# Seven products per block in another order: the v and gate projections of a gated linear attention layer

## The chip, the cores and the metric

One core of a Trainium2 chip runs the whole program. The metric is the device time of one execution in microseconds; the time before is the median of three runs. Below, PE is TensorE, PEld its weight loads, DVE is VectorE, ACT is ScalarE, POOL is GpSimd and SP is SyncE, which issues most loads.

## The reference, cut to what matters

The model has two layers. The first layer's token mixer is a gated linear attention. Its input projection is one large matrix product, of which the change touches two column ranges, v and the gate, each 1024 columns wide:

```
proj = x @ w_in                       # x: 512 x 1024
q, k, v, gate, gk_lr = split(proj, [hk, 2*hk, 2*hk + hv, 2*hk + 2*hv])
o = rms_norm(gla_chunked(q, k, v, g), norm_w)
y = (o * silu(gate)) @ w_out
```

Everything is float32. The kernel keeps float32 accuracy with three products of rounded parts (high x high, low x high, high x low).

## The kernel before, in words

**Seven products instead of eight.** `gated` computes a 512 x 1024 block (v, then the gate) by a scheme of the Strassen-Winograd kind. Tokens, inner dimension and columns are halved, and seven products of sums of quarters replace eight products of quarters. A product's name is that of its weight operand: b11, b21 and b22 are quarters of the weight (row half, column half), t1 to t4 are sums of quarters. The token operand is a quarter of x (a11, a12, a22) or one of four sums (w1, v2, v3, v4) that `x_forms` makes earlier.

**Banks.** Two pairs of PSUM banks accumulate; in a pair, r = 0 and r = 1 are two blocks of 128 tokens. The table `GATED` lists the products in order, each with its token operand and its pair. After the second half of a product, `update` takes each r from its bank: ACT copies it (`copied`), or DVE adds it to, or subtracts it from, a tile already taken out. Some products go on accumulating over what the bank holds already; the others start the bank anew. Either way PE may not write to a bank before `update` has read it. The finished tiles are v or, through a Silu, the gate.

**Halves.** A product comes in two halves (i = 0 and 2), each with its own 128 x 1024 weight tile: 2 x 2 x 3 = 12 matmuls of 128 x 512. The first mixer has 28 such halves, 14 for v and 14 for the gate. They are numbered 0 to 13 here within each part.

**Weights.** A half's raw weight tile is split by ACT into `wh` (a rounding cast, 1.05 us) and then by DVE into `wl` (the rest, 1.2 us). There are four pairs of `wh` and `wl`, so a half's cast can begin only when the half four places earlier has left PE. The raw tiles come in two kinds. The pool `raws` has three slots, shared with every other weight of the program; `gw` has two. A weight sum is made in place: the raw tile, once split, is added to, either by DVE (b11 + b12) or by a transfer from POOL that adds while it writes (`GATED_SUM`). So t1, t2 and t4 are one gw tile in three states, and b22 and t3 are one raw tile in two states. A raw tile that will be added to keeps its slot until the later product has split it.

**What sets the order.** The code issues the halves in the order of `GATED`, each weight a few halves ahead (`look`); a planner with rough costs (`clk`, `vec`) decides where the other work of the mixer (decays, scores, states) is slipped in. Then a scheduler fixes each engine's queue at build time. At run time each queue is strictly in order: an instruction that waits holds up all behind it on its engine.

## Time and profile before

| | us |
|---|---|
| median of three runs | 1223.05 (1222.7 to 1223.29) |
| the profiled execution itself | 1222.6 |
| its span, first to last instruction | 1220.9 |
| PE busy in the span | 1213.7 |
| v halves, first to last matmul | 58.7 to 109.7 |
| gate halves, first to last matmul | 109.9 to 164.1 |

A row of the timeline gives the start, the duration, the engine, the source line, the operation with the tile it writes and those it reads, and in brackets how long the engine was idle before it and who ended that. PE's matmuls are pipelined: a 128 x 512 one is shown as 0.39 us long, but the next starts 0.227 us after it. So a stall on PE is read from the distance of two starts.

### The profile page before, as it was taken

What the parts mean: (1) busy time and instruction counts of PE and PEld (TensorE: products, weight loads), DVE (VectorE), ACT (ScalarE), POOL (GpSimd) and SP (SyncE); (2) the same over time, 40 slices, a digit from 0 to 9 for tenths busy, and PEclk for the clock granted to TensorE, in tenths of its full rate; (3) what the DMA queues carried; (4) which work ended last, traced back from release to release, by engine and by line L of the source; (5) the groups of instructions that cost most, each with busy time, mean ns of one, the idle gap of its engine ahead of it and who ended that gap; (6) DMA issues with size and microseconds to landing.
All of it is one profiled execution on the core that took longest, in us unless ns stands there. A gap on an engine that the chain in (4) does not pass through costs nothing.

```text
span 1220.9 us, 17195 instructions
## 1 busy us (share of the span) xinstructions
PE 1213.7 (99%) x6501; PEld 1024.4 (84%) x6501; DVE 907.4 (74%) x1515; ACT 609.3 (50%) x1072; POOL 161.6 (13%) x203
## 2 busy tenths in 40 slices
PE   9999999999999999999999999999999999999998
PEld 8888888988888888889888888988988888888886
DVE  6989677687757675766789975688687757775667
ACT  5666663644434443454678555544644433443440
POOL 3030101601100110001242030200520100020000
PEclk9999999999999999999999999999999999999999
DMA  8384642535743554433444351335443853383321
GB/s 233 109 165 110 142 143 82 178 116 129 195 125 87 124 100 121 123 102 89 121 128 131 89 136 36 98 110 156 136 123 100 170 179 94 105 178 91 108 65 69
DMA packets 176275, 149.41 MB, mean 122 GB/s; under 512 B 16870, under 2 KB 140842, under 8 KB 176192
## 3 DMA queue, kind: packets, MB, share of 16 engines
q1 hardware_dynamic: 162464, 116.28, 32.3%
q0 software_dynamic: 12768, 31.37, 13.0%
q8 instruction: 51, 0.84, 0.3%
q10 hardware_dynamic: 960, 0.66, 0.2%
q14 instruction: 32, 0.26, 0.1%
HBM read 129.92 MB, written 5.78 MB: 111 GB/s over the span
## 4 chain that ended last, share of the span: by engine, by line
PE 94%; issue 2%; DVE 1%; DMA 1%; ACT 1%; DVEq 0%; POOL 0%; POOLq 0%; ACTq 0%
PE fm L213 55%; PE tm L213 16%; PE fold L213 15%; PE xT L231 1%; DMA gw<-in_gla_w_in_dram 1%; PE o L213 1%; PE pq L213 1%; PE pg L213 1%; PE vn L213 1%; PE yT L231 1%; PE V L213 0%; PE s L213 0%; PE qs L213 0%; PE ks L213 0%; DVE wl L716 0%
## 5 line engine op out<-in xcount | busy, mean ns | idle before, releaser
L213 PE MATMUL fm<-xh,wh 128*128 128x512 f32 (+2 forms) x1096 | 400.3, 368 | 0.7 <-ACT xh L716 0.7
L213 PE MATMUL fm<-xl,wh 128*128 128x512 f32 (+2 forms) x1096 | 398.5, 366 | 0.0
L213 PE MATMUL fm<-xh,wl 128*128 128x512 f32 (+1 forms) x1072 | 391.4, 367 | 0.0
L716 DVE TENSOR_TENSOR wl<-raw,wh 128x1024 fp32r<-128x1024 f32 (+1 forms) x158 | 196.6, 1246 | 150.8 <-ACT wh L716 150.6
L716 ACT CAST wh<-raw 128x1024 fp32r<-128x1024 f32 (+1 forms) x159 | 164.8, 1038 | 210.5 <-PE fm L213 129.0
L213 PEld LDWEIGHTS fm<-xh,wh 128*128 128x128 f32 (+1 forms) x1096 | 205.3, 188 | 33.9 <-ACT xh L716 0.9
L213 PEld LDWEIGHTS fm<-xl,wh 128*128 128x128 f32 (+1 forms) x1096 | 205.4, 188 | 33.1
L213 PEld LDWEIGHTS fm<-xh,wl 128*128 128x128 f32 x1072 | 201.2, 188 | 33.2
L1019 DVE SCALAR_TENSOR_TENSOR conv<-fm,ffn_cw,conv 128x511 f32<-128x511 f32 x112 | 83.5, 746 | 10.0 <-ACT conv L1017 8.3
L213 PE MATMUL fold<-wh,fh 128*128 128x512 f32 x224 | 87.6, 391 | 0.0
L213 PE MATMUL fold<-wh,fl 128*128 128x512 f32 x224 | 87.2, 389 | 0.0
L213 PE MATMUL fold<-wl,fh 128*128 128x512 f32 x224 | 87.1, 389 | 0.0
L716 ACT CAST wh<-b 128x1024 fp32r<-128x1024 f32 x48 | 50.0, 1054 | 74.2 <-PE fold L213 36.8
L716 DVE TENSOR_TENSOR wl<-b,wh 128x1024 fp32r<-128x1024 f32 x48 | 58.2, 1222 | 22.7 <-ACT wh L716 22.4
L412 POOL DMA_DIRECT2D b<-b x24 | 20.8, 902 | 355.0 <-DVE wl L716 304.5
L1037 ACT ACTIVATE conv<-conv 128x512 f32<-128x512 f32 x44 | 27.8, 631 | 64.3 <-DVE conv L1019 64.3
L1574 DVE SCALAR_TENSOR_TENSOR conv<-fm,gdn_cw,conv 128x511 f32<-128x511 f32 (+2 forms) x72 | 54.1, 790 | 5.1 <-ACT conv L1572 4.6
L213 PEld LDWEIGHTS fold<-wh,fh 128*128 128x128 f32 x224 | 42.0, 188 | 9.6 <-DVE h L1108 1.0
L213 PEld LDWEIGHTS fold<-wh,fl 128*128 128x128 f32 x224 | 42.0, 188 | 8.8
L213 PEld LDWEIGHTS fold<-wl,fh 128*128 128x128 f32 x224 | 42.1, 188 | 8.6
L1019 DVE SCALAR_TENSOR_TENSOR form<-fm,ffn_cw,form 128x511 f32<-128x511 f32 x64 | 47.7, 746 | 1.1
L929 POOL TENSOR_TENSOR h<-h,gb 128x512 f32<-128x512 f32 x16 | 24.5, 1547 | 136.4 <-PE xT L231 135.0
(363 smaller groups left out, 2008.7 us busy)
## 6 DMA issues: line engine op xcount, KB each, us to landing
raw<-in_ffn_w_in_dram SPq DMA_DIRECT2D x88, 512.0 KB, 3.9
raw<-in_gdn_w_in_dram SPq DMA_DIRECT2D x32, 512.0 KB, 4.1
b<-in_ffn_w_out_dram SPq DMA_DIRECT2D x24, 512.0 KB, 6.3
b<-b POOLq DMA_DIRECT2D x24, 512.0 KB, 4.7
raw<-in_ffn_w_out_dram SPq DMA_DIRECT2D x20, 512.0 KB, 3.7
raw<-in_gla_w_in_dram SPq DMA_DIRECT2D x18, 512.0 KB, 4.0
gw<-in_gla_w_in_dram POOLq DMA_DIRECT2D x8, 512.0 KB, 7.7
raw<-in_gla_w_out_dram SPq DMA_DIRECT2D x8, 512.0 KB, 3.6
```

What stands on the lines that cost most here:

```text
L213: t = self.nc.tensor.matmul(out, a, b, start=start, stop=stop, skip_group_check=joined)
L231: t = self.nc.tensor.transpose(out, a, self.ident[:n, :n])
L412: self.nc.gpsimd.dma_start(out, group[src, i][:, cols], accum_op=ALU.add)
L716: return self.nc.scalar.copy(dst_h, src), self.nc.vector.tensor_sub(dst_l, src, dst_h)
L929: nc.gpsimd.tensor_mul(h[hf], h[hf], gb[hf])
L1019: nc.vector.scalar_tensor_tensor(a[:, d:], ps[:, :S - d], tap(2 - d), a[:, d:], ALU.mult, ALU.add)
L1037: nc.scalar.activation(a, a, AF.Gelu)
L1574: self.conv = nc.vector.scalar_tensor_tensor(a[:, d:], ps[:, :S - d], tap(3 - d), a[:, d:], ALU.mult, ALU.add)
```

## The change

The order of the seven products goes from b21, b11, t1, b22, t2, t3, t4 (bank pairs 1, 0, 1, 1, 0, 0, 0) to t1, b11, b22, t2, b21, t3, t4 (pairs 1, 0, 1, 0, 1, 0, 0). The first product is now on the sum b11 + b12. So `gated_load` loads b11 into a raw tile and b12 into the gw tile, DVE adds the former to the latter before the first split, and b11 itself is split from the raw tile. b21 comes fifth, on a raw tile of its own. The upper right result is now b11's bank copied by ACT with b21's bank added by DVE; before, b21's was copied and b11's added.

```
-GATED = (("b21", "a12", 1), ("b11", "a11", 0), ("t1", "w1", 1), ("b22", "v4", 1), ("t2", "v2", 0), ("t3", "v3", 0),
+GATED = (("t1", "w1", 1), ("b11", "a11", 0), ("b22", "v4", 1), ("t2", "v2", 0), ("b21", "a12", 1), ("t3", "v3", 0),
          ("t4", "a22", 0))
...
     def gated_load(self, group, name, i):
...
+        def load(quarter, t):
+            self.nc.sync.dma_start(t.rearrange("p (j f) -> p j f", j=2), self.gated_rows(group, quarter, i))
+            group[quarter, i] = t
+
+        raw = lambda: self.rp.tile([P, 1024], F32, name=self.uid("raw"), tag="raw")
+        if name == "t1":
+            load("b11", raw())
+            load("b12", self.mp.tile([P, 1024], F32, name=self.uid("gw"), tag="gw", bufs=2))
+        elif name in ("b22", "b21"):
+            load(name, raw())
 
     def issue_gated(self, group, name, i):
         nc = self.nc
         t = group[GATED_IN[name], i]
         if name == "t1":
-            nc.vector.tensor_add(t, t, group.pop((name, i)))
+            nc.vector.tensor_add(t, t, group["b11", i])
...
-        if name in ("b21", "t3", "t4"):
+        if name in ("b11", "b21", "t3", "t4"):
             del group[GATED_IN[name], i]
...
-            if name == "b21":
-                top[r] = copied(x)
+            if name == "t1":
+                high[r] = copied(x)
             elif name == "b11":
-                nc.vector.tensor_add(top[r], top[r], p)
-                done(r, 1, top[r], top[r])
-            elif name == "t1":
-                high[r] = copied(x)
+                top[r] = copied(p)
...
+            elif name == "b21":
+                nc.vector.tensor_add(top[r], top[r], x)
+                done(r, 1, top[r], top[r])
```

Of PE's queue, the matmuls are the same in kind and number. The queues of DVE and ACT are rearranged from the end of the q and k projections to the output projection. Two places matter for what follows.

The first is DVE's queue in the v part, from the split of half 8 on. There, `na`, `z`, `bc` and the `e` tiles belong to the decays of a head; `wl` rows are splits; `v` rows with `fold` are `update`. Before, half 8 and 9 are t2's (gw), 10 and 11 are t3's (raw):

```order
L716 TENSOR_TENSOR wl_911<-gw_661,wh_910 128x1024
L1360 SCALAR_TENSOR_TENSOR na_905<-z_904 128x512
L1364 SCALAR_TENSOR_TENSOR z_904<-z_904,na_905 128x512
L1366 SCALAR_TENSOR_TENSOR bc_949<-reset_83,z_904 128x512
L716 TENSOR_TENSOR wl_932<-gw_709,wh_931 128x1024
L1371 TENSOR_TENSOR e_176_951<-bc_949 128x512
L716 TENSOR_TENSOR wl_957<-raw_775,wh_956 128x1024
```

Now half 8 and 9 are b21's, both on raw tiles (raw_869 and raw_892):

```order
L717 TENSOR_TENSOR wl_915<-raw_869,wh_914 128x1024
L1361 SCALAR_TENSOR_TENSOR na_909<-z_908 128x512
L1365 SCALAR_TENSOR_TENSOR z_908<-z_908,na_909 128x512
L1367 SCALAR_TENSOR_TENSOR bc_951<-reset_83,z_908 128x512
L1372 TENSOR_TENSOR e_178_953<-bc_951 128x512
L717 TENSOR_TENSOR wl_935<-raw_892,wh_934 128x1024
L717 TENSOR_TENSOR wl_959<-raw_757,wh_958 128x1024
```

The same seven kinds of rows stand there; one split now reads a tile, raw_892, whose load can be issued only when the slot of raw_869 is free, that is behind the first row, since b22's two raw tiles hold the other two slots until t3 is split. A little further on, DVE's queue before ends t2's and t3's turns like this (v_966 and v_974 are t2's subtractions, v_921 and v_929 are t3's):

```order
L1235 TENSOR_TENSOR v_966<-v_966,fold_741 128x512
L716 TENSOR_TENSOR wl_1005<-gw_661,wh_1004 128x1024
L1235 TENSOR_TENSOR v_974<-v_974,fold_742 128x512
L716 TENSOR_TENSOR wl_1025<-gw_709,wh_1024 128x1024
L1394 TENSOR_TENSOR e_185_995<-e_185_995,qk_655 128x4x64
L1395 TENSOR_TENSOR e_185_995<-e_185_995,qk_601 128x4x64
L1360 SCALAR_TENSOR_TENSOR na_1074<-z_1073 128x512
L1397 TENSOR_TENSOR bc_949<-bc_949,qk_601 128x512
L1238 TENSOR_TENSOR v_921<-v_921,fold_741 128x512
```

Now b21's additions (v_877 and v_885) stand in that place, t2's subtractions have gone up the queue, and t3's (v_784, v_792) follow:

```order
L717 TENSOR_TENSOR wl_1005<-gw_611,wh_1004 128x1024
L1390 COPY dec_1000<-bc_951 128x4
L1236 TENSOR_TENSOR v_877<-v_877,fold_747 128x512
L1236 TENSOR_TENSOR v_885<-v_885,fold_748 128x512
L717 TENSOR_TENSOR wl_1027<-gw_615,wh_1026 128x1024
L1394 TENSOR_TENSOR e_184_992<-e_184_992,qk_659 128x512
L1395 TENSOR_TENSOR e_185_995<-e_185_995,qk_659 128x4x64
L1396 TENSOR_TENSOR e_185_995<-e_185_995,qk_601 128x4x64
L1239 TENSOR_TENSOR v_784<-v_784,fold_745 128x512
```

Two rows of the decays (`na`, and `bc` times q) moved behind t3's subtractions, and two `v` rows came in ahead of them.

The second place is ACT's queue in the gate part, at halves 8 to 10 and the copies of the transposed keys (`kt`), which PE's `ds` matmuls read. Before, with t2's halves on gw tiles:

```order
L716 CAST wh_1326<-gw_1063 128x1024
L1220 COPY sg_1337<-fold_1214 128x512
L1220 COPY sg_1345<-fold_1215 128x512
L716 CAST wh_1347<-gw_1129 128x1024
L716 CAST wh_1433<-raw_1246 128x1024
L1425 COPY kt_1399<-kt_1394 128x512
```

Now, with b21's halves on raw tiles, raw_1290 and raw_1314:

```order
L717 CAST wh_1328<-raw_1290 128x1024
L1221 COPY sg_1338<-fold_1218 128x512
L1221 COPY sg_1346<-fold_1219 128x512
L717 CAST wh_1348<-raw_1314 128x1024
L717 CAST wh_1433<-raw_1228 128x1024
L1426 COPY kt_1399<-kt_1394 128x512
```

The `kt` copies stand, as before, behind the casts of halves 9 and 10; the cast of half 9 now reads a tile whose load is issued only after DVE's split of half 8 (raw_1290 to `wl`).

More of the change, by code (lines that the diff above doesn't have):

```diff
@@ L32 @@
 FOLD = [(n, FOLD_NEW[n], *FOLD_ALL[n]) for n in ("b11", "b21", "t1", "t2", "b22", "t3", "t4")]
-GATED = (("b21", "a12", 1), ("b11", "a11", 0), ("t1", "w1", 1), ("b22", "v4", 1), ("t2", "v2", 0), ("t3", "v3", 0),
+GATED = (("t1", "w1", 1), ("b11", "a11", 0), ("b22", "v4", 1), ("t2", "v2", 0), ("b21", "a12", 1), ("t3", "v3", 0),
          ("t4", "a22", 0))
-GATED_NEW = {"b21": "b21", "b11": "b11", "t1": "b12", "b22": "b22"}
-GATED_IN = {"b21": "b21", "b11": "b11", "t1": "b11", "b22": "b22", "t2": "b11", "t3": "b22", "t4": "b11"}
+GATED_IN = {"t1": "b12", "b11": "b11", "b22": "b22", "t2": "b12", "b21": "b21", "t3": "b22", "t4": "b12"}
 GATED_SUM = {"t1": "b22", "b22": "b12", "t2": "b21"}
@@ L438, in gated_load @@
     def gated_load(self, group, name, i):
-        if name not in GATED_NEW:
-            return
-        if name == "b11":
-            t = self.mp.tile([P, 1024], F32, name=self.uid("gw"), tag="gw", bufs=2)
-        else:
-            t = self.rp.tile([P, 1024], F32, name=self.uid("raw"), tag="raw")
-        self.nc.sync.dma_start(t.rearrange("p (j f) -> p j f", j=2), self.gated_rows(group, GATED_NEW[name], i))
-        group[name, i] = t
+        def load(quarter, t):
[7 more added lines that the diff above has]
+            load(name, raw())
     def issue_gated(self, group, name, i):
```

## The prediction

> **What bounds the kernel now.** I read the page's busy times and chain first, then the two parts that the change touches as windows, then what PE waited for in them.

> ```profile
> span 1220.9 us, 17195 instructions
> PE 1213.7 (99%) x6501; PEld 1024.4 (84%) x6501; DVE 907.4 (74%) x1515; ACT 609.3 (50%) x1072; POOL 161.6 (13%) x203
> PE 94%; issue 2%; DVE 1%; DMA 1%; ACT 1%; DVEq 0%; POOL 0%; POOLq 0%; ACTq 0%
> ...
> 58.00:112.00 54.00, 53.61 (x280) 44.33 (x279) 47.69 (x81) 36.65 (x66) 11.06 (x13) 1.00 0.66 150
> 112.00:164.00 52.00, 51.42 (x283) 42.65 (x282) 41.83 (x103) 35.10 (x64) 7.09 (x6) 1.00 0.46 102
> ...
> PE fold L213 <- DVE sg L1235: 0.4, 1, 0.4
> PE fold L213 <- DVE v L1235: 0.4, 1, 0.4
> ```

> PE is the bound: 99% busy, and 94% of the chain that ended last. The windows (length, then PE, PEld, DVE, ACT, POOL busy, clock, DMA share) show the v part and the gate part: the granted clock is 1.00, PE is idle for 0.39 and 0.58 us, and DVE is the next busiest with 47.69 of 54 and 41.83 of 52. The last two rows are all that PE is shown to have waited for there: DVE's subtraction of t2's bank, once in each part. Since PE's work stays the same, the change can win only PE's stalls in these two parts and lose only what it adds to them.

> **What it removes.** PE's rows around the four places where a half must wait for a bank of its own pair (v: t2 to t3, t1 to b22; gate: t1 to b22, t2 to t3):

> ```profile
> 79.53 0.39 PE L213 MATMUL fold<-wh,xfl 128*128 128x512 f32 x1
> 79.77 0.50 PE L213 MATMUL fold<-wh,xfh 128*128 128x512 f32 x1
> 80.11 0.40 PE L213 MATMUL fold<-wl,xfh 128*128 128x512 f32 x1
> ...
> 89.42 0.39 PE L213 MATMUL z<-lr,gk 96*128 96x512 f32 x1
> 90.20 0.47 PE L213 MATMUL fold<-wh,xfh 128*128 128x512 f32 x1 [0.39 <-DVE v L1235]
> 90.51 0.40 PE L213 MATMUL fold<-wl,xfh 128*128 128x512 f32 x1
> ...
> 126.03 0.39 PE L213 MATMUL fold<-wh,xfl 128*128 128x512 f32 x1
> 126.56 0.50 PE L213 MATMUL fold<-wh,xfh 128*128 128x512 f32 x1
> 126.90 0.40 PE L213 MATMUL fold<-wl,xfh 128*128 128x512 f32 x1
> ...
> 150.35 0.71 PE L231 MATMUL yT<-ident,sg 128*128 128x128 f32 x5
> 151.50 0.50 PE L213 MATMUL fold<-wh,xfh 128*128 128x512 f32 x1 [0.43 <-DVE sg L1235]
> 151.83 0.39 PE L213 MATMUL fold<-wl,xfh 128*128 128x512 f32 x1
> ```

> Steps between starts are 0.227 us where nothing waits (rows of 0.39 overlap). Three rows span two steps, 0.45: 79.53 to 80.11 has 0.13 too much, 89.42 to 90.51 has 0.63, 126.03 to 126.90 has 0.41. Behind the transposes, 0.43 idle and 0.33 instead of 0.23 make about 0.6 with the slow first steps. In the new order another product stands between each of these pairs, so the wait has 5.4 us of other matmuls (24 x 0.227) for cover. The sum is 1.8 us, all of it on PE's path. The new queue of PE has one `ds` matmul on its own ahead of t4's first half, one more change between the two kinds; the row at 134.69 further down shows such a first matmul behind `ds` as 0.58 long instead of 0.39, so I put it at 0.2. Net 1.6 us to win, no more: t3 to t4 stays in one pair.

> **What hides at no cost.** The sum b11 + b12 is made before half 0 now; its raw tile is loaded where b21's was.

> ```profile
> 50.47 1.22 DVE L716 TENSOR_TENSOR wl<-raw,wh 128x1024 fp32r<-128x1024 f32 x1
> ...
> 58.70 0.39 PE L213 MATMUL fold<-wh,xh 128*128 128x512 f32 x1
> ```

> Before, the split of half 1 ended at 51.7, and PE began half 0 at 58.70: 7 us of cover for two additions of the same width, 2.4 us. If that cover were gone, each 1 us of lateness would be 1 us of PE. The adding transfers on POOL get one product more between the split that frees them and their use. Evictions are equal in number: ACT copies as often, DVE adds as often.

> **What it adds: a load that stands behind a split.** b21 comes while b22's two raw tiles hold two of three slots. So its second half's load is issued on SP only when DVE has split the first, and that split needs half 4 to have left PE. For v, the rows of before that stand at this point:

> ```profile
> 75.67 1.05 ACT L716 CAST wh<-gw 128x1024 fp32r<-128x1024 f32 x1 [1.67 <-PE fold L213]
> ...
> 76.75 1.22 DVE L716 TENSOR_TENSOR wl<-gw,wh 128x1024 fp32r<-128x1024 f32 x1 [1.49 <-ACT wh L716]
> 80.37 0.69 DVE L1364 SCALAR_TENSOR_TENSOR z<-z,na 128x512 f32<-128x512 f32 x1 [1.79 <-ACT na L1362]
> 81.10 1.22 DVE L1366 TENSOR_TENSOR_SCAN bc<-reset,z 128x512 f32<-128x512 f32 x1
> 82.24 1.20 DVE L716 TENSOR_TENSOR wl<-gw,wh 128x1024 fp32r<-128x1024 f32 x1
> 83.36 0.68 DVE L1371 TENSOR_TENSOR e<-bc 128x512 f32<-128x512 f32 x1
> 83.96 1.22 DVE L716 TENSOR_TENSOR wl<-raw,wh 128x1024 fp32r<-128x1024 f32 x1
> 94.72 0.68 DVE L1238 TENSOR_TENSOR v<-v,fold 128x512 f32<-128x512 f32 x1
> ...
> 95.77 0.39 PE L213 MATMUL fold<-wh,xh 128*128 128x512 f32 x1
> ```

> Half 8 is cast at 75.67 and split by 76.75 + 1.22 = 77.97, now as before. The load goes out at 78.0 and lands L later; ACT's cast takes 1.05, so DVE can start half 9's split at 79.1 + L. DVE itself gets to that row at 82.84: z at 80.37, then 0.73, 1.14 and 0.60 (the distances z to scan, scan to the next, and e to the next). So DVE's queue, and all behind it, is late by L - 3.7. From z to t3's first subtraction DVE ran without a gap (80.37 to 94.72, 14.35 us), and the new queue has the same sum: two 512-wide rows of the decays out, two of `update` in. So t3's subtraction ends at 94.72 + 0.68 + (L - 3.7), and t4, in the same pair, cannot start before. PE would be there at 95.77 - 0.13 - 0.63 + 0.43 (`ds` moved ahead; three of them take 1.21 from 133.48 on, below) = 95.44, where the subtraction of before ended at 95.40: no slack; with 0.1 for the hand-over, **wait A is L - 3.6.**

> L is read from the transfers of 512 KB around (median us to landing; windows at 59, 85, 88.5, 118 and 77 to 79 us):

> ```profile
> raw<-in_gla_w_in_dram SPq DMA_DIRECT2D x1, 512.0 KB, 3.5
> ...
> raw<-in_gla_w_in_dram SPq DMA_DIRECT2D x1, 512.0 KB, 5.6
> ...
> raw<-in_gla_w_in_dram SPq DMA_DIRECT2D x1, 512.0 KB, 4.8
> ...
> raw<-in_gla_w_out_dram SPq DMA_DIRECT2D x1, 512.0 KB, 6.7
> ...
> gw<-in_gla_w_in_dram POOLq DMA_DIRECT2D x1, 512.0 KB, 8.5
> ```

> A load alone took 3.5; one issued while an adding transfer of POOL was under way took 4.8 to 6.7. At 78.0 t2's two adding transfers are under way (issued behind the splits of halves 6 and 7, and taking up to 8.5), so I take 5.6, the row with the most alike neighbours, and keep 3.5 and 6.7 as ends. A is 2.0, from 0 to 3.1. Half 9 itself is in time: split by 85.9 with L = 5.6, needed at 86.6 (one half, 12 x 0.227, before the 89.3 of t3 that is worked out below). [...]

> In the gate part the same load stands ahead of the `kt` copies on ACT.

> ```profile
> 123.54 0.39 PE L213 MATMUL fold<-wh,xfh 128*128 128x512 f32 x1
> ...
> 131.90 1.05 ACT L716 CAST wh<-raw 128x1024 fp32r<-128x1024 f32 x1 [3.03 <-PE fold L213]
> 132.85 1.07 ACT L1425 COPY kt<-kt 128x512 f32<-128x512 f32 x2
> ...
> 133.48 1.56 PE L213 MATMUL ds<-v,kt 128*128 128x256 f32 x6
> 134.69 0.58 PE L213 MATMUL fold<-wh,xfl 128*128 128x512 f32 x1
> ```

> Half 4 leaves PE at 123.54. Cast and split take 1.05 and 1.22, the hand-overs some 0.3 (an estimate), so the load is issued at 126.1 and lands at 126.1 + L. Two casts follow, 0.95 apart (131.90 to 132.85), then `kt` at 128.05 + L. Before it was at 132.85, less half 6's 0.41 that is gone: 132.44. PE's `ds` stands right behind that copy already (it began at 133.48, 0.1 late by the steps). **Wait B is L - 4.4**: 1.2 with 5.6, from 0 to 2.3. In the gate part eight transposes stand between t3 and t4 on PE, so A is not repeated there.

> **The sum:** -1.8 + 0.2 + 2.0 + 1.2 = +1.6 us. On the profiled execution's 1222.6 that is 1224.2; the median of the runs shown lies 0.45 above it, so 1224.6.

> **The rivals.**
> *The loads come quickly* (L up to 4.4, near the lone 3.5): A is 0 to 0.8, B nothing, and the time is 1221.4 to 1222.3. For it: one of the two adding transfers may be nearly through at 78. Against it: every load beside one took 4.8 or more. 25%. [...]
> *The loads come slowly*, the other side: by the sum, +2L - 9.6, the kernel is slower by more than 2.4 us from L = 6.0 on. With 6.7 it is -1.6 + 3.1 + 2.3 = +3.8, so 1226.9. For it: a 6.7 row, at the start of a bunch of POOL's transfers, and two of them under way here. 25%.
> *It does not do what it says:* the waits for banks stay, because DVE's queue puts t2's subtractions late wherever the product stands. They stand behind two splits now, so the first starts at 82.84 + 1.9 + 2 x 1.13 = 87.0 and ends at 87.7; PE needs it at 89.3 (90.20 less 0.55, 0.13 and the `z` matmul's 0.23, which moves behind t3). That is 1.6 us of cover, so against it. Then the 1.8 stays and A and B come on top: +3.4, 1226.4; 5%.
> *Something gives more than these waits:* no row of the two parts holds more; 5% for a gain over 2.4.

> **How the numbers follow.** 0.2% of 1223.05, 2.4 us, is about what a measurement tells from no change. The forecast (L from 4.4 to 6.0, 1222.3 to 1225.5) has 40%. No change is that and the quick loads, 0.65; slower is the slow loads and the waits that stay, 0.30; faster 0.05. The range goes from a gain of the full 1.8, less the 0.3 by which runs differ (1220.9), to the slow loads' 1226.9 with the 0.2 of spread (1227.1).

> **What would show it.** In the profile after: no wait of PE for the t2 subtraction; a wait of PE for DVE's subtraction of t3's bank at t4 in v, near 95.4 to 97.5 us; DVE idle ahead of half 9's split near 83 us, ended by a cast; ACT idle ahead of the cast of half 9 in the gate part near 131 us, ended by a load; PE waiting for `kt`. The prediction is wrong if b21's second load lands within 4 us, or if another row, at half 0 or at the states of t4, becomes a wait.

## The result: 9 us slower, and the profile after

The changed kernel takes 1232.15 us (median of five, 1230.83 to 1233.14) against 1223.05 (also of five): ratio 1.0074, 95% interval 1.0063 to 1.0086. The forecast was 1224.6, its range 1220.9 to 1227.1. The profiled execution is the one of 1232.15 us. First its page: span, busy times, chain.

```profile
span 1230.4 us, 17192 instructions
PE 1217.4 (99%) x6501; PEld 1028.2 (84%) x6501; DVE 907.3 (74%) x1515; ACT 609.3 (50%) x1072; POOL 161.2 (13%) x203
PE 96%; DVE 2%; DMA 1%; ACT 1%; issue 0%; DVEq 0%; POOL 0%; ACTq 0%; POOLq 0%
```

The span is 9.5 us longer, yet PE counts only 3.7 us more of busy time. The page can't tell more; the two parts can. The windows of the v part and the gate part:

```profile
58.00:112.00 54.00, 52.05 (x266) 43.12 (x265) 43.23 (x63) 31.99 (x52) 10.49 (x12) 0.97 0.62 139
112.00:164.00 52.00, 47.47 (x249) 39.48 (x248) 36.12 (x104) 31.99 (x65) 4.72 (x4) 0.93 0.44 105
```

PE is idle for 1.95 and 4.53 us (0.39 and 0.58 before), and the granted clock, 1.00 in both before, is 0.97 and 0.93. Both matter. What PE waited for from 58 to 164 us, all of it (total, times, longest):

```profile
PE ds L212 <- DVE sc L1442: 4.5, 1, 4.5
PE fold L212 <- DVE v L1239: 1.9, 1, 1.9
```

The waits for t2's subtractions are gone, as the change promised. Two new ones stand in their place, and both come from one cause: b21's second load. First the v part, in the timeline:

```profile
83.78 2.00 ACT L717 CAST wh<-raw 128x1024 fp32r<-128x1024 f32 x2 [3.27 <-DMA raw<-in_gla_w_in_dram]
...
84.86 2.36 DVE L717 TENSOR_TENSOR wl<-raw,wh 128x1024 fp32r<-128x1024 f32 x2 [1.64 <-ACT wh L717]
...
96.88 1.28 DVE L1239 TENSOR_TENSOR v<-v,fold 128x512 f32<-128x512 f32 x2
...
95.17 0.59 PE L212 MATMUL ds<-v,kt 128*128 128x256 f32 x2
97.71 0.47 PE L212 MATMUL fold<-wh,xh 128*128 128x512 f32 x1 [1.95 <-DVE v L1239]
98.02 0.47 PE L212 MATMUL fold<-wl,xh 128*128 128x512 f32 x1
98.29 0.63 PE L212 MATMUL fold<-wh,xl 128*128 128x512 f32 x1
98.72 0.63 PE L212 MATMUL fold<-wh,xh 128*128 128x512 f32 x1
...
101.34 0.71 PE L212 MATMUL fold<-wh,xh 128*128 128x512 f32 x1
101.89 0.40 PE L212 MATMUL fold<-wl,xh 128*128 128x512 f32 x1
102.13 0.40 PE L212 MATMUL fold<-wh,xl 128*128 128x512 f32 x1
```

This is wait A: ACT waits for the load, DVE for ACT's cast; DVE's queue runs late, t3's subtraction frees its bank at 97.6, and t4 stands until 97.71, 2.2 us longer than a step would be. Then something that the prediction doesn't contain: the steps are 0.43 us instead of 0.227 (98.29 to 98.72) and become 0.24 only at 101.89. Summed over the steps from 97.7 to 101.9, that is 1.6 us more.

The gate part:

```profile
137.95 1.99 ACT L717 CAST wh<-raw 128x1024 fp32r<-128x1024 f32 x2 [7.68 <-DMA raw<-in_gla_w_in_dram]
...
139.02 1.23 DVE L717 TENSOR_TENSOR wl<-raw,wh 128x1024 fp32r<-128x1024 f32 x1 [4.96 <-ACT wh L717]
139.84 1.06 ACT L1426 COPY kt<-kt 128x512 f32<-128x512 f32 x2
...
140.28 0.44 DVE L1442 COPY_PREDICATED sc<-gla_mask,sa 64x256 f32<-64x256 uint8 x1
...
140.84 0.29 PEld L212 LDWEIGHTS ds<-v,kt 128*128 128x128 f32 x1 [4.94 <-ACT kt L1426]
140.87 0.77 PE L212 MATMUL ds<-v,kt 128*128 128x256 f32 x1 [4.53 <-DVE sc L1442]
...
143.99 0.63 PE L212 MATMUL fold<-wh,xfh 128*128 128x512 f32 x1
144.42 0.63 PE L212 MATMUL fold<-wl,xfh 128*128 128x512 f32 x1
```

This is wait B: 4.7 us more than a step. The weight load of `ds` waits for ACT's `kt` copy, as foreseen; the matmul also waits for DVE's last `sc` copy, which stands behind half 9's split and reads a bank that `ds` needs. Of the two, `sc` ends last: the first of the two `kt` copies, the one that `ds` starts on, ends at 140.42, `sc` at 140.72. Both stand behind the same load. The steps are 0.43 again up to 146.0; that is 2.4 us more.

Now the load itself, as transfers: the answer for 77.5 to 78.5 us (v), that for 129 to 130 us (gate), and the bytes by queue while each load was under way (78.2 to 83.8, 129.3 to 137.9):

```profile
raw<-in_gla_w_in_dram SPq DMA_DIRECT2D x1, 512.0 KB, 5.6
...
raw<-in_gla_w_in_dram SPq DMA_DIRECT2D x1, 512.0 KB, 8.6
...
DMA packets 577, 1.08 MB, mean 193 GB/s; under 512 B 48, under 2 KB 48, under 8 KB 577
...
q0 software_dynamic: 305, 0.56, 62.0%
q1 hardware_dynamic: 272, 0.52, 24.5%
...
DMA packets 860, 1.64 MB, mean 191 GB/s; under 512 B 64, under 2 KB 64, under 8 KB 859
...
q0 software_dynamic: 587, 1.10, 70.9%
q1 hardware_dynamic: 272, 0.52, 17.8%
```

The same 0.52 MB on SP's queue (q1) took 5.6 us beside 0.56 MB of POOL's adding transfers (q0), and 8.6 us beside 1.10 MB. Averaged over the time of the load, all of it together went at about 192 GB/s both times. Within that time it is uneven: up to 81.0 us in v and 132.3 us in the gate part, 2.8 and 3.0 us after the issue, the same view shows no packet of the load, only POOL's; from 133.3 to 135.3 us it shows 120 of the load's and 129 of POOL's.

The bill of the profiled execution: 0.2 us later at half 0 (58.92 against 58.70), 3.0 in the v part (-0.8 + 2.2 + 1.6), 5.9 in the gate part (-1.0 + 4.7 + 2.4 is 6.1), 0.4 later on: 9.5.

### The profile page after: what moved, and what is told of

It reads as the page before. It is cut to its first block, busy times and chain, and to the rows that moved or that the text cites. A ratio compares the mean times of both kernels' runs of the same rounds, so it can differ in the third digit from the quotient of the medians.

```text
span 1230.4 us, 17192 instructions
## 1 busy us (share of the span) xinstructions
PE 1217.4 (99%) x6501; PEld 1028.2 (84%) x6501; DVE 907.3 (74%) x1515; ACT 609.3 (50%) x1072; POOL 161.2 (13%) x203
## 4 chain that ended last, share of the span: by engine, by line
PE 96%; DVE 2%; DMA 1%; ACT 1%; issue 0%; DVEq 0%; POOL 0%; ACTq 0%; POOLq 0%
PE fm L212 54%; PE fold L212 17%; PE tm L212 16%; PE o L212 2%; DMA raw<-in_gla_w_in_dram 1%; PE xT L230 1%; PE pq L212 1%; PE pg L212 1%; PE vn L212 1%; PE ds L212 1%; PE yT L230 1%; DVE wl L717 1%; PE V L212 0%; PE qs L212 0%; PE s L212 0%; PE ks L212 0%
## 5 line engine op out<-in xcount | busy, mean ns | idle before, releaser
L717 DVE TENSOR_TENSOR wl<-raw,wh 128x1024 fp32r<-128x1024 f32 (+1 forms) x162 | 200.4, 1240 | 158.2 <-ACT wh L717 157.9
L717 ACT CAST wh<-raw 128x1024 fp32r<-128x1024 f32 (+1 forms) x163 | 168.8, 1039 | 214.1 <-PE fm L212 131.9
L212 PE MATMUL fold<-wh,fh 128*128 128x512 f32 x224 | 87.7, 391 | 0.0
L717 DVE TENSOR_TENSOR wl<-b,wh 128x1024 fp32r<-128x1024 f32 x48 | 58.3, 1223 | 22.6 <-ACT wh L717 22.4
## 6 DMA issues: line engine op xcount, KB each, us to landing
raw<-in_ffn_w_in_dram SPq DMA_DIRECT2D x88, 512.0 KB, 3.9
raw<-in_gdn_w_in_dram SPq DMA_DIRECT2D x32, 512.0 KB, 4.1
b<-in_ffn_w_out_dram SPq DMA_DIRECT2D x24, 512.0 KB, 6.0
b<-b POOLq DMA_DIRECT2D x24, 512.0 KB, 4.6
raw<-in_ffn_w_out_dram SPq DMA_DIRECT2D x20, 512.0 KB, 3.7
raw<-in_gla_w_in_dram SPq DMA_DIRECT2D x18, 512.0 KB, 4.5
gw<-in_gla_w_in_dram POOLq DMA_DIRECT2D x8, 512.0 KB, 6.6
raw<-in_gla_w_out_dram SPq DMA_DIRECT2D x8, 512.0 KB, 3.6
```

The costliest lines, as they stand in the source:

```text
L212: t = self.nc.tensor.matmul(out, a, b, start=start, stop=stop, skip_group_check=joined)
L717: return self.nc.scalar.copy(dst_h, src), self.nc.vector.tensor_sub(dst_l, src, dst_h)
```

## Experiment 1: a tile of its own for b21's second half

```
-GLA_SLOTS = 47
+GLA_SLOTS = 45
...
+        elif name == "b21" and i:
+            load(name, self.mp.tile([P, 1024], F32, name=self.uid("gx"), tag="gx", bufs=1))
         elif name in ("b22", "b21"):
             load(name, raw())
```

> The second half of b21 gets a tile of its own, so that its load is issued with the one of the first half; the 4 KB come from two of the 47 slots. Theory (the load stood behind DVE's split of b21's first half for want of a raw slot, and all of the loss follows from that): waits A and B go, the granted clock is 1.00 in both parts again, and what is left is the 1.8 us of bank waits that the new order takes away: 1221.5 us (1221.0 to 1222.3). Rival (the new order's evictions or the adding transfers make the loss, whatever the slot): 1228 to 1232 us.

Measured: 1221.69 us (11 runs, 1220.98 to 1222.2) against 1222.89; ratio 0.999, interval 0.9981 to 0.9999. The windows and PE's only wait in them:

```profile
58.00:112.00 54.00, 53.49 (x281) 44.46 (x280) 46.52 (x78) 35.59 (x63) 10.50 (x12) 1.00 0.67 153
112.00:164.00 52.00, 52.00 (x288) 43.66 (x287) 42.12 (x106) 36.17 (x68) 4.71 (x4) 1.00 0.40 93
```

```profile
PE fold L212 <- DVE v L1241: 0.5, 1, 0.5
```

The whole loss, 10.5 us, hung on the slot; the new order of products and evictions itself costs nothing that these views show. In the gate part PE has no idle time left; in v, t4 waits 0.5 us for t3's subtraction. This version beats both kernels by the measured medians, the one before by 0.1%, an interval that just excludes no change.

## Experiment 2: the new order in one part alone

In each of these two kernels one part uses the tables, loads and `update` of before; the second has `sg`, the gate part's tag, in the place of `v`.

```
-        for name, form, at in GATED:
+        for name, form, at in GATED if tag == "v" else GATED_OLD:
```

> New order in the v part, old order in the gate part. Theory (two separate losses): the v part costs 2.2 us of wait A and 1.6 us of slow clock, less 0.8 of bank waits, with 0.2 ahead of half 0: about +3.1, 1226.1 us (1225.3 to 1227.0). Rival (the gate part's loss is the v part's, carried on: the queues come late into the gates): most of the 9 us, 1229 to 1232 us.

> Old order in the v part, new order in the gate part. Theory (two separate losses): 4.7 us of wait B and 2.5 us of slow clock, less 1.0 of bank waits: about +6, 1229 us (1228 to 1230). Rival (the gate part's loss is carried over from the v part): no loss here, 1222 to 1223.5 us.

Measured: v alone 1224.96 (11 runs, 1223.81 to 1226.85; ratio 1.0018, 1.0009 to 1.0027), gates alone 1226.49 (5 runs, 1225.91 to 1229.55; 1.0037, 1.0024 to 1.0049), before 1222.89. So each part loses by itself, +2.1 and +3.6, less than I had expected and less together than the 9.1 of both. One reason is in the profile: with the gates alone, b21's second load took 7.7 us instead of 8.6, and PE stood for 3.7 instead of 4.5. Another shows in the single executions. Of v alone, six had a mean granted clock of 1.000 and took 1223.8 to 1225.0; five had 0.999 and took 1225.4 to 1226.9. Of the gates alone, three had 0.999 and took 1225.9 to 1226.5; two had 0.997 and took 1228.9 and 1229.6. That reads as a wait that is always there and slow steps that come in some executions and not in others: some 1.4 us and then 1.9 more for v, 3.2 and then 3.1 more for the gates. The rounded clock alone doesn't prove it: 0.999 also stands on seven of the 21 executions of the kernel before that were taken beside these, at 1222.6 to 1222.9 us, so the two kinds of v rest on their times, and whether the three of the gates at 0.999 had some slow steps is open. The four sum to 9.6; the changed kernel, whose five executions are all at 0.996 or 0.997, stands at 9.1.

## Experiment 3: the adding transfers out of the load's way

The first try only wrote t2's two transfers later in the code, behind b21's second split:

> The changed kernel, with t2's two adding transfers issued behind b21's second split instead of behind t2's own splits; b21's second load still stands behind b21's first split. Theory (that load takes 5.6 and 8.6 us because it lands only when the adding transfers ahead of it are through): it lands within 5 us in both parts, wait A falls from 2.2 to under 1.4, wait B from 4.7 to under 0.7, the clock is 1.00: 1222.5 us (1221.3 to 1224.5). Rival 1 (a load at this place takes so long whatever POOL's transfers do): 1230 to 1233 us. Rival 2 (the sums come too late for t4): the load is quick, but t4's casts wait for a transfer, 1225 us or more.

Measured: 1231.47 (5 runs; ratio 1.0068, 1.0055 to 1.008), as the changed kernel. It moved nothing. Nothing stands ahead of these transfers in POOL's queue, so they were issued as soon as t2's splits were through, at 72.9 and 76.0 us (73.1 and 76.2 in the changed kernel), and b21's second load took 5.4 us in v (5.6 in the changed kernel), while in the gate part PE's idle time ahead of `ds` was 4.54 us (4.53). Its profiled execution shows one thing more, in the window of the v part:

```profile
58.00:112.00 54.00, 52.19 (x274) 43.40 (x274) 44.79 (x71) 33.91 (x56) 10.49 (x12) 1.00 0.65 147
```

t4 waits here as well (1.8 us of idle PE), but the clock is 1.00 and the steps behind the wait are 0.23. From half 0 to the first gate matmul this execution takes 52.5 us, the changed kernel's 54.2. Of the 1.8 us between them (before rounding), 0.1 is a shorter wait; the rest, 1.6, is what the slow steps cost there.

In the second try the transfers stand behind a copy on POOL that reads b21's second split:

```
+        if name == "b21" and i:
+            mark = nc.gpsimd.tensor_copy(self.small([P, 1], "mark", bufs=2), wl[:, :1].bitcast(F32))
+            for k in (0, 2):
+                self.behind(adding("t2", k), mark)
```

> The changed kernel, with t2's two adding transfers really held back: POOL first copies one column of b21's second split, and the transfers stand behind that copy in its queue. b21's second load still stands behind b21's first split. Theory (that load lands only when the adding transfers ahead of it are through): with only b22's transfers ahead it lands within 5 us in both parts, wait A is under 1.4 instead of 2.2, wait B under 0.8 instead of 4.7, the clock 1.00 in the gate part: 1223 us (1221.3 to 1225), and if the held sums come late for t4 in the v part, that shows as a cast waiting for a transfer. Rival (the load takes 5.6 to 8.6 us at this place whatever POOL's transfers do): 1230 to 1233 us.

Measured: 1235.23 (4 runs; ratio 1.01, 1.0085 to 1.0115). The time is outside what either theory gave, but the trace answers the question. The load in both parts (78 to 79 and 134 to 135 us), the held transfers in v (85 to 88 us):

```profile
raw<-in_gla_w_in_dram SPq DMA_DIRECT2D x1, 512.0 KB, 3.6
...
raw<-in_gla_w_in_dram SPq DMA_DIRECT2D x1, 512.0 KB, 3.4
...
gw<-in_gla_w_in_dram POOLq DMA_DIRECT2D x2, 512.0 KB, 9.6
```

The load takes 3.6 and 3.4 us in the very places where it took 5.6 and 8.6. Its first packet is shown 1.0 us after the issue in both parts. So the adding transfers made it long, and the rival is out. And in the gate part the wait is gone. The v part pays in another place (ACT's timeline, then PE's):

```profile
94.12 1.05 ACT L725 CAST wh<-gw 128x1024 fp32r<-128x1024 f32 x1 [7.63 <-DMA gw<-in_gla_w_in_dram]
...
102.46 0.76 PE L212 MATMUL fold<-wh,xh 128*128 128x512 f32 x1 [5.72 <-DVE v L1247]
```

Issued at 86 instead of 73 and 76, the sums come too late for t4's cast, and t4 stands for 5.7 us: in v there is no room on either side. From the last gate matmul to the end this kernel also takes 4.5 us longer than the changed one, in several stretches; the cause of that is open.

## Experiment 4: PE kept busy in the waits

Matmuls whose results nobody reads fill the two waits: 9 ahead of t4 in v, 19 ahead of `ds` in the gate part.

```
+                    if tag == "v" and not i:
+                        for _ in range(9):
+                            nc.tensor.matmul(acc[1][0], self.xh[:, 0, :P], self.xh[:, 0, :S], start=True, ...)
...
+            if hd == 2:
+                for _ in range(19):
+                    nc.tensor.matmul(pd[0], self.xh[:, 0, :P], self.xh[:, 0, :S], start=True, ...)
```

> The changed kernel, with 9 matmuls of 128x512 into an unused bank ahead of t4 in the v part and 19 into the bank of ds ahead of ds in the gate part: PE works through the two waits (2.0 and 4.3 us), and their results are overwritten or never read. Theory (the slow steps behind the waits come from PE's idleness): the granted clock is 1.00 throughout, steps stay 0.227, both waits end when they did: 1232.15 less 1.6 and 2.5, 1228.1 us (1227.3 to 1229.0). Rival (the slow steps come from something that goes on at that time, a transfer or another engine's work): no change, 1231.5 to 1233 us.

Measured: 1235.98 (4 runs; ratio 1.0103, 1.0088 to 1.0119), slower instead of faster. In v the steps stayed at 0.23. In the gate part the 19 themselves waited (their row in PE's timeline):

```profile
140.78 1.62 PE L1471 MATMUL ds<-xh 128*128 128x512 f32 x3 [4.41 <-DVE sc L1446]
```

They don't use `kt` at all, so this shows that the bank of `ds` is itself held by DVE's `sc` until then, and they were run at the slow steps on top. The second try sends them to b22's pair, which has been read by that time:

> As the run before with PE filled in the waits, but the 19 matmuls ahead of ds in the gate part go to the bank pair of b22, which has been read by then, so that they don't wait for the bank of ds themselves. Theory (the clock falls since PE is idle): granted clock 1.00 in both parts; the gate part loses its 4.7 us of wait and no slow steps, 2.5 us less than in the changed kernel; the v part loses as in the first filled run (3.3 us at its end): 1229.7 us (1228.8 to 1230.8). Rival (the clock falls for another reason): slow steps of 0.427 us in the gate part again, 1231.5 to 1236 us.

Measured: 1229.01 (4 runs, 1228.87 to 1229.21; ratio 1.0049, 1.0036 to 1.0063). The gate part in PE's timeline, and the windows of both parts:

```profile
135.82 4.60 PE L1472 MATMUL fold<-xh 128*128 128x512 f32 x19
140.26 1.46 PE L212 MATMUL ds<-v,kt 128*128 128x256 f32 x6
141.37 0.58 PE L212 MATMUL fold<-wh,xfh 128*128 128x512 f32 x1
141.78 0.39 PE L212 MATMUL fold<-wl,xfh 128*128 128x512 f32 x1
142.01 0.39 PE L212 MATMUL fold<-wh,xfl 128*128 128x512 f32 x1
```

```profile
58.00:112.00 54.00, 52.73 (x274) 43.05 (x274) 44.51 (x73) 33.24 (x54) 10.49 (x12) 1.00 0.66 152
112.00:164.00 52.00, 52.00 (x283) 43.67 (x282) 37.47 (x99) 32.65 (x66) 4.71 (x4) 1.00 0.40 92
```

With useless work in the waits, as long as they are, the clock is 1.00 and the kernel 3.1 us quicker than the changed one. So it was PE's idleness that brought the slow steps here. It is not the whole 4.0, for the added matmuls also changed the queues that the scheduler built: in v, PE now stands for DVE's states behind t4 (0.4 us in the waits of this run, some 1.3 by the steps), which it doesn't do in experiment 3's first try, at full clock too. What is left, 1229.0 against 1222.9, is the waits, now filled. (The row of `ds` shows no idle time of PE ahead of it, so the 19 matmuls lasted at least as long as the wait that they fill.)

## Experiment 5: waits made on purpose

On the kernel of experiment 1, where no load is late. Two tries put four operations of DVE or one, which change nothing, ahead of t3's subtraction:

> The kernel with b21's second half in a tile of its own (1221.7 us), with four more 128x512 operations of DVE (which change nothing) ahead of t3's first subtraction in the v part: a made wait of PE at t4, 0.7 + 4 x 0.6 = 3.1 us long. Theory (a PE idle of 2 us or more brings the slow clock, whatever caused it): steps of 0.427 us behind it for some 3.4 us in most executions, 2.4 + 1.6: 1225.7 us (1224.5 to 1226.5). Rival (only waits for a transfer do it): no slow steps, 1224.1 us (1223.5 to 1224.5).

> The same with one more operation: a made wait of 0.7 + 0.6 = 1.3 us. Theory: too short for the clock to fall, no slow steps in any execution, 1222.3 us (1221.8 to 1222.9). Rival (any stop of PE over a microsecond brings the slow clock): 1223.5 us or more.

Measured: 1221.68 and 1221.74 (10 runs each), no change: these operations needed only ready data and ran earlier, in DVE's idle time. They tell nothing of the clock. The next two kernels read the bank itself, twice or once, and the subtraction stands behind these reads:

```
+                if tag == "v" and not r:
+                    read = self.slot("read")
+                    for _ in range(2):
+                        self.read = nc.vector.tensor_copy(read, p)
                 self.third = nc.vector.tensor_sub(high[r], high[r], p)
```

> The kernel with b21's second half in a tile of its own, with two more copies by DVE out of t3's bank ahead of t3's first subtraction in the v part (results unused; an addition of 1.1 us that came later slips in between): a made wait of PE at t4 of about 2.6 us with no transfer behind it. Theory (a PE idle of more than 2 us brings the slow clock in some executions, by where it falls): executions of two kinds, 1223.9 us at a granted clock of 1.000 and 1225.5 at 0.999. Rival (only the waits for the load do it): all at 1.000, 1223.5 to 1224.3 us.

> The same with one copy: a made wait of about 0.9 us. Theory: too short for the clock to fall in any execution, 1222.0 us (1221.6 to 1222.6). Rival (any stop of PE of about a microsecond brings the slow clock): executions of 1223.5 us and more.

Measured: with two 1223.97 (10 runs, 1222.94 to 1225.5; ratio 1.001, 1.0 to 1.0019), with one 1221.34 (10 runs, 1220.73 to 1222.07; 0.9988, 0.9978 to 0.9997). The wait in PE's timeline with two, then with one:

```profile
98.29 0.47 PE L212 MATMUL fold<-wh,xh 128*128 128x512 f32 x1 [1.96 <-DVE v L1245]
```

```profile
96.73 0.47 PE L212 MATMUL fold<-wh,xh 128*128 128x512 f32 x1 [0.24 <-DVE v L1245]
```

PE's idle of 2.0 us (2.2 by the steps) gives executions of two kinds: five at 1222.9 to 1223.4 with a clock of 1.000, five at 1224.6 to 1225.5 with 0.998. With the short one (0.5 us by the steps) none of ten shows a second kind. The times of the two kinds lie some 0.6 us under what I expected; the split is as the theory has it.

## Why the prediction was wrong, by its steps

- **What it removes, 1.8 us:** right. None of the four stalls is left, and experiment 1, where only 0.5 us of new waiting takes their place, gains 1.2.
- **What hides at no cost:** right. The additions of b11 and b12 delay nothing; half 0 starts 0.2 us later, and over the kernels of this document that start varies by 0.6 (58.6 to 59.2).
- **Wait A = L - 3.6:** right. L was 5.6, as taken, which gives 2.0; PE lost 2.2. That L fits so closely is partly luck: in v alone (experiment 2) this load took 5.8 us, in experiment 3's first try 5.4.
- **Wait B = L - 4.4:** the formula held, L didn't. With 8.6 it gives 4.2, measured 4.7 (the rest came through DVE's `sc`, which the prediction had not seen behind half 9's split). The step that failed is the one that read L once, "from the transfers of 512 KB around", and used it for both parts, with 6.7 as its upper end. The adding transfers stood closer together in the gate part, so that twice as many bytes of them were still to come (1.10 MB against 0.56); the row of 8.5 us for an adding transfer, quoted there, would have been the better end. That is 3.0 us for L and 0.5 for `sc`.
- **PE's work stays the same:** that step failed too. The sum counted what PE would wait and nothing of what the wait does to the steps behind it: 1.6 and 2.4 us in the profiled execution; experiment 3's first try confirms the 1.6, and filling the waits won 3.1 net of what it added. No row of the profile before shows it, where the longest stop of PE in these parts was 0.43 us.
- **The rivals:** the slow loads were the right mechanism, with too low a price: 1226.9. How the load and the adding transfers share the way is shown for the gate part from 133.3 to 135.3 us: 120 packets of the load to 129 of POOL's. In the first 2.8 and 3.0 us of the two loads only POOL's packets are shown; why the load's began so late is open. With the adding transfers held (experiment 3) its first packet came 1.0 us after the issue, and it took 3.6 and 3.4 us, near the 3.5 of a load alone in the profile before.

Forecast +1.6, measured in the profiled execution +9.5. Of the 7.9 between them, 3.0 are L in wait B, 0.7 the other misses of the two waits, 4.0 the slow steps and 0.6 lie outside the two parts; these make 8.3, 0.4 too much: the 0.2 that the forecast set aside for the single `ds` matmul has no counterpart in the bill, and the terms of the gate part add up to 0.2 more than its own length.

## What to carry to other kernels

A load that can be issued only when a slot comes free is priced with the bytes that are already queued when it goes out, at that place, and not with the landing times of loads elsewhere: here (0.52 MB + what POOL still had to move) / 192 GB/s fits both parts. That quotient is an average and no rate of the hardware: in the profile before it is 208 GB/s for the load issued at 85.2 us (5.6 us) and 177 for the one issued at 118.3 (6.7 us), and for the load with the adding transfers held (experiment 3) 142 and 152. A stop of PE can cost more than its length: the two in the profiled execution, of 2.2 and 4.7 us by the steps, cost 1.6 and 2.4 us on top, and one of 2.2 us in experiment 5 some 1.8 us in five of ten executions; one of 0.5 us there showed no such cost in ten. And before an order is changed for the sake of banks, count the raw tiles that are alive at each step in the new order: one tile too few undid it, and one tile more made it a gain.
